# Three modulation vectors by matmuls in column quarters instead of sums on VectorE

## The chip, the cores and the metric

The kernel runs on one core of a Trainium2 chip. The metric is the device time of one execution, in microseconds (us); lower is better. PE is TensorE, DVE VectorE, ACT ScalarE, POOL GpSimd and SP the engine that issues most loads. "Before" is the kernel that the change starts from.

## The reference, cut to what matters

Two transformer blocks are computed for 512 tokens of width 1024. The first block takes a conditioning vector `c` and makes six modulation vectors of 1024 numbers from it. They shift, scale and gate what the attention and the expert layer see:

```python
c_act = jax.nn.silu(c)
mod = c_act @ w_ada[l] + b_ada[l]                  # 1024 x 6144 weights
sh_a, sc_a, g_a, sh_f, sc_f, g_f = jnp.split(mod, 6, axis=-1)
h = modulate(rmsnorm(x), sh_a, sc_a)               # h * (1 + scale) + shift
...                                                # windowed and latent attention
x = x + g_a[:, None, :] * (mixed @ w_out[l])
h = modulate(rmsnorm(x), sh_f, sc_f)
x = x + g_f[:, None, :] * peer(h, ...)
```

So `sh_a` and `sc_a` are needed at once, `g_a` (vector 2) at the output projection, `sh_f` and `sc_f` (3 and 4) at the norm behind it, and `g_f` (5) only at the end of the expert layer. All is fp32; most matmuls are made of three fp32r products of a split into a high and a low part (`mm3`, lines 199 to 201).

## The kernel before, in words

The tile `mod`, 128 x 48, holds the six vectors as columns: column m is numbers 128 m to 128 m + 127, eight columns to a vector. Each column is made on DVE. A row block of the transposed weights, 128 x 1024 (512 KB, the tile `wa`), is loaded by SP (`ada_dma`, line 491); one instruction multiplies it by the broadcast `silu(c)` in `cs` and sums along the row into the column (line 553 for columns 0 to 15, line 503 for the other 32). The bias is added later, a vector or more at a time (lines 738, 772, 817).

Columns 16 to 47 are made beside other work by the generator `ada_rest` (line 494). Each step of it issues one load and sums the tile loaded a step earlier, with two buffers; the sum is held behind the latest row maximum or up-projection product on DVE. `next(ada)` takes a step. The stages around it, in order:

- The latent up-projection (lines 642 to 664): eight query tiles `qu` of six 128x512 matmuls, eight `kup` of three and four `vup` of three, into eight PSUM banks that are used in turn. DVE multiplies each query tile by a table (line 649); the rotary part of the first attention's queries is done beside it, with copies by DMA. A step of `ada` after every second query tile.
- The first, windowed attention (`attend`, line 241, with names that begin with sw): 32 units, each a score tile, a row maximum on DVE, an exponential on ACT, a scaling on POOL, a transpose and, for two units together, the product with the values (line 329, `128*64`: each head of a pair writes one half of the output partitions). A step of `ada` after every eighth unit (`ADA_E`). `ps.then(sc=LA + 1, pt=2, po=5 - LA)` (line 666) hands the eight banks on, the one used longest ago first: five to scores, two to transposes, one to outputs.
- The second, latent attention (names with ml): the same 32 units with scores of 128x512 in fp32 (line 269). Beside it weights of the output projection are loaded and split, and `both` (line 728) takes a step of `ada` after every second of those steps. What is left of the 24 columns is made at the end (line 737).
- The output projection (`w_out`, line 751): two halves of four row blocks, each block 24 matmuls, then a scaling by `out_rstd` and `ga` and an addition to `x` on DVE (lines 761 and 762). `ga` is vector 2 as a row, made by `mod_row` (line 212). Two steps of `ada` a block, for columns 40 to 47; in the second half the norm of the block before follows (`norm2`, line 794), which transposes on PE and needs vectors 3 and 4.

Loads wait for a free buffer on SP's queue, in order; weights for `mm3` come through `Stream` (line 79) with four raw buffers, split on ACT and DVE (lines 111 and 112). The order on each engine is settled when the program is built, by a scheduler that goes by program order and by when it takes an instruction to be ready; the engine then works its queue in that order.

Of the kernel before, what the change touches and what calls it, by code (L numbers as in the profile page):

```python
# [9 lines left out]
FT = mybir.dt.float32  # L10
# [10 lines left out]
P = 128  # L21
# [24 lines left out]
GSCALE = 4096.0  # L46
WR, WH, SD = 4, 5, 3
RB = 1
ADA_E = 8
ADA1 = 40  # L50
LA = 4
ADA_U = 2
ADA_M = 2
OGP = 3
U_PRE = 4
B_END = 120
# [101 lines left out]
def body(ctx, tc, a):  # L158
# [3 lines left out]
    def pool(st, name, bufs=1, side="left", **kw):  # L162
        return st.enter_context(tc.tile_pool(name=name, bufs=bufs, side=side, reuse_waits="tile", **kw))
# [304 lines left out]
    rp = ExitStack()  # L468
    crow = cs[0:1]
    nc.sync.dma_start(crow, a["c"])  # L470
    i = A.activation(crow, crow, AF.Silu)
    with tc.issue_after(i.ins):

        A.activation(small.tile([P, 1], FT, name="warm0", tag="nss"), eps, AF.Sqrt)
# [14 lines left out]
    def ada_dma(pl, m, eng, bufs):  # L489
        wa = pl.tile([P, D], FT, name=f"wa{m}", tag="wa", bufs=bufs)  # L490
        eng.dma_start(wa, a["w_adaT"][m * P:(m + 1) * P, :])
        return wa

    def ada_rest(pl, ms, bufs=2):

        prev = []
        for m in list(ms) + [None] * (bufs - 1):
            if m is not None:
                prev.append((m, ada_dma(pl, m, nc.sync, bufs)))
            if m is None or len(prev) == bufs:  # L500
                n, w = prev.pop(0)
                with tc.issue_after(last["max"]):
                    V.scalar_tensor_tensor(w, w, 1.0, cs, op0=OP.mult, op1=OP.mult, accum_out=mod[:, n:n + 1])
            yield

    with ExitStack() as s1:
# [132 lines left out]
                    V.tensor_copy(km[64:, h], t[64:])  # L639


        ada = ada_rest(pada, range(16, ADA1))
        for h in range(8):
            if h % 2 == 0:
                w = ws.get(("qup", h // 2))
            pt = ps.tile([P, S], FT, name=f"qu{h}", tag="ps")
            c = slice(h % 2 * 256, h % 2 * 256 + 256)
            lin(pt, [(w[0][:, c], w[1][:, c])], 2, ALL, lambda k: lT[:, 0, k], lambda k: lT[:, 1, k])
            last["max"] = V.tensor_mul(qm[:, h], pt, tabm[:, 0]).ins
            if h % ADA_U == 0:  # L650
                next(ada, None)
        for h in range(8):
            if h % 4 == 0:
                w = ws.get(("kup", h // 4))
            pt = ps.tile([P, S], FT, name=f"kup{h}", tag="ps")
            c = slice(h % 4 * P, (h % 4 + 1) * P)
            mm3(pt, w[0][:, c], w[1][:, c], lT[:, 0, 2], lT[:, 1, 2], True, True)
            A.activation(km[:64, h], pt[:64], AF.Copy)
        w = ws.get(("vup",))
        for b in range(NB):  # L660
            pt = ps.tile([P, 512], FT, name=f"vup{b}", tag="ps")
            bl = slice(b * P, (b + 1) * P)
            mm3(pt, lT[:, 0, 2, bl], lT[:, 1, 2, bl], w[0], w[1], True, True)
            A.activation(vm[:, b], pt, AF.Copy)

    ps = ps.then(sc=LA + 1, pt=2, po=5 - LA)
    fa = ExitStack()
    pc = pool(fa, "pc", 2)

    def attn_done(half, pl):  # L670
        st = {}
# [27 lines left out]
    def zip_run(main, side, every=1):  # L699
        n = 0  # L700
        for _ in main:
            n += 1
            if n % every == 0:
# [5 lines left out]
                   lambda kt, h: va[:, kt, (h // 4) * 64:(h // 4) * 64 + 64],  # L709
                   [(j, j + 4) for j in range(4)], 64 ** -0.5, "sw", attn_done(0, pc),  # L710
                   mask=(identb, maskb), sink=vec[:, V_SINK:V_SINK + 8]), ada, ADA_E)
    fa.close()
    rq.close()
    r1 = ExitStack()
# [10 lines left out]

    wol = wo_loads()

    def both():
        while True:
            for i in range(ADA_M):  # L730
                next(wol, None)
                yield
            next(ada, None)
    zip_run(attend(pc, ps, lambda h: (qm[:, h], None), lambda h: (km[:, h], None),
                   lambda kt, h: vm[:, kt, h * 64:(h + 1) * 64],
                   [(2 * j, 2 * j + 1) for j in range(4)], 96 ** -0.5, "ml", attn_done(1, pc)), both())
    run(wol, ada)
    V.tensor_add(mod[:, 16:24], mod[:, 16:24], vec[:, V_BADA + 16:V_BADA + 24])
    fa.close()
    rp.close()  # L740

# [4 lines left out]
    ga = pd1.tile([P, D], FT, name="ga")  # L746
    mod_row(ps, "ps", ga, 16, "ga")
    rows_tiles(pd1, "wo", range(4, 8))
    ada = ada_rest(pd1, (*range(ADA1, 48),))

    def w_out(half, b):
        bl = slice(b * P, (b + 1) * P)
# [13 lines left out]
    for b in range(NB):  # L766
        take_rows("wo", 4 + b)
        next(ada, None)
        next(ada, None)
        w_out(0, b)  # L770
    next(ada, None)
    V.tensor_add(mod[:, 24:40], mod[:, 24:40], vec[:, V_BADA + 24:V_BADA + 40])
    V.tensor_scalar(mod[:, 32:40], mod[:, 32:40], 1.0, None, op0=OP.add)
    out_rstd[1] = out_rstd[1]("ps")
    r1.close()
# [15 lines left out]
    with ExitStack() as s2:  # L791
        pn = pool(s2, "pn", 2)

        def norm2(b):
            sq = pn.tile([P, D], BF, name=f"sq2{b}", tag="sq", bufs=1)
            ss = small.tile([P, 1], FT, name=f"ss2{b}", tag="nss")
            A.activation(sq, x[:, b], AF.Square, accum_out=ss)
            r = rstd(ss, 1, 1.0 / D, f"n2{b}")
            xn = pn.tile([P, D], FT, name=f"xn2{b}", tag="xn")
            V.tensor_scalar(xn, x[:, b], r, None, op0=OP.mult)  # L800

            def dst(k0, b=b):
                c = slice(b * P, (b + 1) * P)
                return hA[:, 0, k0:k0 + 4, c], hA[:, 1, k0:k0 + 4, c]
            transposed(pn, ps, xn, dst, mod[:, 32:40], mod[:, 24:32], f"n2{b}",
                       lambda k0: G if b < 3 and k0 == 0 else V)

        for b in range(NB):
            w_out(1, b)
            if b:  # L810
                norm2(b - 1)
            next(ada, None)
            next(ada, None)
        ws.upto(("qy", 0, 1), 0)
        norm2(NB - 1)
    run(ada)
    V.tensor_add(mod[:, 40:48], mod[:, 40:48], vec[:, V_BADA + 40:V_BADA + 48])
    s1.close()
    rm.close()

# [697 lines left out]
def _layout(inp):  # L1518
    i = {k: np.asarray(v) for k, v in inp.items()}
    con, tab = _constants()  # L1520
    wi = i["w_in"][0]
    qa, ka, va, ql, kvl, kr = np.split(wi, np.cumsum([512, 128, 128, 256, 128]), axis=1)
    order = np.concatenate([np.arange(h * 64, h * 64 + 64) for j in range(4) for h in (j, j + 4)])
    z64 = np.zeros((D, 64), wi.dtype)
    w_in = np.concatenate([ql, kvl, va, z64, kr, kr, ka, qa[:, order]], axis=1)
    qup = i["w_mla_q_up"][0].reshape(256, 8, 96)
    rp = qup[:, :, 64:]
    qup = np.concatenate([qup, rp[:, :, 16:], rp[:, :, :16]], axis=2).reshape(256, 1024)
    kvu = i["w_mla_kv_up"][0].reshape(128, 8, 128)
    kup = np.concatenate([kvu[:, :, :64], np.zeros_like(kvu[:, :, :64])], axis=2).reshape(128, 1024)  # L1530
    vup = kvu[:, :, 64:].reshape(128, 512)
    wi2 = i["w_in_2"][0]
    q2, k2, v2, u2 = np.split(wi2, [512, 640, 768], axis=1)

    half = np.arange(64).reshape(2, 2, 16).transpose(1, 0, 2).reshape(64)
    q2 = q2[:, order].reshape(D, 8, 64)[:, :, half].reshape(D, 512)
    k2 = k2.reshape(D, 2, 64)[:, :, half].reshape(D, 128)
    w_in2 = np.concatenate([q2, k2, v2, u2], axis=1)
    vecs = np.concatenate([
        _cols(i["b_ada"][0]), _cols(i["mla_q_norm"][0]), _cols(i["mla_kv_norm"][0]),  # L1540
        _cols(i["out_norm_swa"][0][order]), _cols(i["out_norm_mla"][0]), _cols(i["norm1_g_2"][0]),
        np.tile(i["q_norm_g_2"][0][half], 2)[:, None], np.tile(i["k_norm_g_2"][0][half], 2)[:, None],
        _cols(i["pool_b_2"][0]), _cols(i["pool_scale_2"][0]), _cols(i["norm2_g_2"][0]),
        np.broadcast_to(i["swa_sink"][0][None, :], (P, 8)),
    ], axis=1)
    assert vecs.shape == (P, NVEC)
    return {
        "x": i["x"][0], "c": i["c"], "vecs": vecs, "consts": con, "tabs": tab,
        "w_adaT": i["w_ada"][0].T, "w_in": w_in,
        "w_qup": _rows(_pack(qup)), "w_kup": kup, "w_vup": vup, "w_out": np.concatenate([i["w_out"][0][:512][order], i["w_out"][0][512:]], axis=0),  # L1550
        "w_query": _pack(i["w_peer_query"][0]),
        "subT": i["peer_sub_keys"][0].reshape(16, P, P).transpose(2, 0, 1).reshape(P, 2048),
        "uT": _pack(i["peer_expert_u"][0].T), "u": i["peer_expert_u"][0], "v": i["peer_expert_v"][0], "final_norm": i["final_norm"][None, :],
        "w_in2": _pack(w_in2), "pool_w": i["pool_w_2"][0], "w_out2": np.concatenate([i["w_out_2"][0][:512][order], i["w_out_2"][0][512:]], axis=0),
        "w_gate": _pack(i["w_gate_2"][0]), "w_up": _pack(i["w_up_2"][0]), "w_down": i["w_down_2"][0],
    }
# [17 lines left out]
```

## Time and profile before

| | |
|---|---|
| median of 3 runs | 2220.59 us (2214.14 to 2221.76) |
| the profiled execution | 2222.11 us |
| its span in the profile | 2220.3 us |
| busy: PE, PEld, DVE, ACT, POOL | 95%, 80%, 73%, 43%, 28% |
| mean granted clock of PE | 0.977 |
| HBM traffic | 366.66 MB read, 4.19 MB written |

The profile is one execution, taken by the hardware profiler. Its span runs from the first to the last instruction, and the execution's own time is 1.8 us longer. PE is busy with matmuls, PEld with loading their stationary operand, which overlaps. An fp32 matmul leaves two records in the trace, an fp32r one a single record. A row of a timeline or of a group names line, engine, operation, the tile written `<-` the tiles read, the columns of the array where PE is concerned (`128*64` is 128 rows and 64 columns), and the idle time before it with what ended it. The stages told above lie between 62 and 294 us of the 2220.

### The profile page before, as it was taken

What the parts mean: (1) busy time and instruction counts of PE and PEld (TensorE: products, weight loads), DVE (VectorE), ACT (ScalarE), POOL (GpSimd) and SP (SyncE); (2) the same over time, 40 slices, a digit from 0 to 9 for tenths busy, and PEclk for the clock granted to TensorE, in tenths of its full rate; (3) what the DMA queues carried; (4) which work ended last, traced back from release to release, by engine and by line L of the source; (5) the groups of instructions that cost most, each with busy time, mean ns of one, the idle gap of its engine ahead of it and who ended that gap; (6) DMA issues with size and microseconds to landing.
All of it is one profiled execution on the core that took longest, in us unless ns stands there. A gap on an engine that the chain in (4) does not pass through costs nothing.

```text
span 2220.3 us, 35038 instructions
## 1 busy us (share of the span) xinstructions
PE 2102.8 (95%) x12443; PEld 1771.4 (80%) x12443; DVE 1624.1 (73%) x3587; ACT 954.2 (43%) x1899; POOL 618.3 (28%) x553
## 2 busy tenths in 40 slices
PE   7999998888999999999999999999998999999999
PEld 5756787778888888888888888788887678888887
DVE  7779889997878997777799777777767865333322
ACT  4467342345435553333355433333353553333321
POOL 2245245564222113333312233333303420000000
PEclk9999999988999999999999999999999999999999
DMA  8515522231575558878855688888844221333332
GB/s 273 166 49 164 173 70 66 89 111 57 172 254 191 168 166 270 281 268 285 285 186 165 196 279 268 262 265 281 295 138 122 65 67 45 98 96 99 95 117 73
DMA packets 163634, 375.79 MB, mean 169 GB/s; under 512 B 18562, under 2 KB 22530, under 8 KB 163459
## 3 DMA queue, kind: packets, MB, share of 16 engines
q1 hardware_dynamic: 121058, 233.81, 31.6%
q0 software_dynamic: 36864, 134.23, 19.3%
q10 hardware_dynamic: 5536, 5.51, 0.9%
q8 instruction: 98, 1.61, 0.3%
q14 instruction: 78, 0.63, 0.1%
HBM read 366.66 MB, written 4.19 MB: 167 GB/s over the span
## 4 chain that ended last, share of the span: by engine, by line
PE 56%; DVE 16%; DMA 15%; issue 6%; ACT 4%; POOL 2%; ACTq 0%; SPq 0%; DVEq 0%; POOLq 0%
DMA vr<-in_v_dram,idx 7%; PE vac L200 4%; PE vac L201 4%; PE vac L199 4%; PE pA L199 4%; PE pA L200 4%; PE pA L201 3%; DMA wr<-in_uT_dram 3%; DMA ur<-in_u_dram,idx 3%; PE pd L201 2%; PE pd L200 2%; PE pd L199 2%; PE upp L201 2%; PE upp L199 2%; PE upp L200 2%
## 5 line engine op out<-in xcount | busy, mean ns | idle before, releaser
L111 ACT ACTIVATE wh<-wr 128x512 fp32r<-128x512 f32 x716 | 446.8, 631 | 760.4 <-DMA wr<-in_v_dram 162.1
L112 DVE TENSOR_TENSOR wl<-wr,wh 128x512 fp32r<-128x512 f32 x640 | 429.4, 695 | 286.4 <-ACT wh L111 270.2
L200 PE MATMUL vac<-wl,wwh 128*128 128x512 f32 x756 | 305.4, 404 | 32.7 <-DVE wl L112 32.3
L199 PE MATMUL pA<-hA,wh 128*128 128x384 f32 x928 | 318.1, 343 | 0.0
L201 PE MATMUL pA<-hA,wl 128*128 128x384 f32 x928 | 314.7, 339 | 0.0
L200 PE MATMUL pA<-hA,wh 128*128 128x384 f32 x928 | 313.9, 338 | 0.0
L199 PE MATMUL vac<-wh,wwh 128*128 128x512 f32 x756 | 304.3, 403 | 0.7 <-ACT wwh L1042 0.5
L201 PE MATMUL vac<-wh,wwl 128*128 128x512 f32 x756 | 299.5, 396 | 0.1
L1067 POOL DMA_INDIRECT ur<-in_u_dram,idx x128 | 160.5, 1254 | 383.3 <-DVE acc L1078 308.2
L1067 POOL DMA_INDIRECT vr<-in_v_dram,idx x128 | 155.3, 1213 | 338.2 <-DVE ur L1070 252.5
L200 PEld LDWEIGHTS vac<-wl,wwh 128*128 128x128 f32 x756 | 144.2, 191 | 73.5 <-DVE wl L112 49.2
L1078 DVE SCALAR_TENSOR_TENSOR acc<-vr,act,acc 128x1024 f32<-128x1024 f32 x127 | 162.7, 1281 | 46.7 <-DMA vr<-in_v_dram,idx 45.4
L1070 DVE SCALAR_TENSOR_TENSOR ur<-ur,hn 128x1024 f32<-128x1024 f32 x128 | 156.2, 1220 | 39.0 <-DMA ur<-in_u_dram,idx 39.0
L199 PEld LDWEIGHTS pA<-hA,wh 128*128 128x128 f32 x928 | 177.0, 191 | 4.1 <-ACT ga L1031 0.7
L200 PEld LDWEIGHTS pA<-hA,wh 128*128 128x128 f32 x928 | 177.0, 191 | 3.1
L201 PEld LDWEIGHTS pA<-hA,wl 128*128 128x128 f32 x928 | 176.6, 190 | 0.0
L201 PEld LDWEIGHTS vac<-wh,wwl 128*128 128x128 f32 x756 | 144.0, 190 | 30.1 <-DVE wwl L1043 0.8
L199 PEld LDWEIGHTS vac<-wh,wwh 128*128 128x128 f32 x756 | 144.1, 191 | 28.7 <-ACT wh L111 0.9
L112 POOL TENSOR_TENSOR wl<-wr,wh 128x512 fp32r<-128x512 f32 x76 | 101.9, 1352 | 74.6 <-ACT wh L111 71.7
L1042 ACT ACTIVATE wwh<-w 128x384 fp32r<-128x384 f32 x126 | 66.0, 524 | 117.2 <-DVE w L1035 115.0
L1008 PEld LDWEIGHTS <-oj 128*128 128x128 f16 x1152 | 83.2, 117 | 38.1 <-issue 16.4
L989 DVE TENSOR_TENSOR oj<-iT,ioth 128x1024 f16<-128x1024 f16 x144 | 106.0, 740 | 9.2 <-PE pG L1009 9.2
(697 smaller groups left out, 4319.7 us busy)
## 6 DMA issues: line engine op xcount, KB each, us to landing
wr<-in_uT_dram SPq DMA_DIRECT2D x256, 256.0 KB
wr<-in_v_dram SPq DMA_DIRECT2D x256, 256.0 KB
wa<-in_w_adaT_dram SPq DMA_DIRECT2D x48, 512.0 KB
wr<-in_w_gate_dram SPq DMA_DIRECT2D x44, 256.0 KB
wr<-in_w_up_dram SPq DMA_DIRECT2D x44, 256.0 KB
wr<-in_w_down_dram SPq DMA_DIRECT2D x44, 256.0 KB
wr<-in_w_in_dram SPq DMA_DIRECT2D x36, 256.0 KB
wr<-in_w_out_dram SPq DMA_DIRECT2D x32, 256.0 KB
```

Of the source, the lines that this page charges most:

```text
L111: self.nc.scalar.activation(hi, raw, AF.Copy)
L112: (lo_eng or self.nc.vector).tensor_tensor(lo, raw, hi.bitcast(FT), op=OP.subtract)
L199: T.matmul(out, lh, rh, start=start, stop=False)
L200: T.matmul(out, lh, rl, start=False, stop=False)
L201: return T.matmul(out, ll, rh, start=False, stop=stop).ins
L989: V.tensor_tensor(out, iT[:, q, tt].rearrange("p (s t) -> p s t", t=4)[:, :, None].to_broadcast([P, GS // 4, w, 4]), ioth[:, None, j0:j0 + ...
L1008: T.matmul(pt[:, t, :n], oj[:, t // 4, :, t % 4], o[:, :, 1], start=True, stop=False)
L1042: A.activation(wh, w, AF.Copy)
L1067: G.indirect_dma_start(out=r, out_offset=None, in_=a[kind], in_offset=bass.IndirectOffsetOnAxis(ap=idx[:, j:j + 1], axis=0))
L1070: V.scalar_tensor_tensor(r, r, 1.0, hn, op0=OP.mult, op1=OP.mult, accum_out=act[:, j:j + 1])
L1078: V.scalar_tensor_tensor(acc, r, act[:, j:j + 1], acc, op0=OP.mult, op1=OP.add)
```

## The change

`ada_pe` makes vectors 2, 3 and 5 on PE. For a half of a vector (512 numbers) it loads eight tiles of the weights as they are, 128 x 512 (256 KB, tile `wv`), and multiplies each with a column of `silu(c)` spread to 32 columns as the stationary operand. Four tiles at a time go to the four quarters of 32 output partitions of one bank (a group, `g` from 0 to 3); a second group adds to it. ACT copies the bank to a row tile, and four matmuls against a 128 x 1 column `sel`, with ones at rows 0, 32, 64 and 96, add up the quarters and turn the row into four columns of `mod` (here called flips); DVE adds the bias. A half takes three steps of the generator: group, group and copy, flips. There are five `wv` buffers, and the row takes one of them as well. Vectors 2 and 3 are made in the up-projection, with a step after each query tile and every second `kup` tile and the last one behind `vup`; vector 5 is made in the output projection with one step a block. Vector 4 (columns 32 to 39) stays on DVE and is made in the first attention, a step after every fourth unit; the second attention has none.

```diff
-ADA_E = 8
-ADA1 = 40
+ADA_E = 4
...
+    ccol = keep.tile([P, KD], FT, name="ccol")
+    nc.scalar.dma_start(ccol, a["c_cols"])
     i = A.activation(crow, crow, AF.Silu)
+    i = A.activation(ccol, ccol, AF.Silu)
+    sel = keep.tile([P, 1], FT, name="sel")
+    V.memset(sel, 0.0)
+    for g in range(4):
+        V.memset(sel[32 * g:32 * g + 1], 1.0)
...
+    def ada_pe(pl, tag, vs, bufs=4):
+        todo = [(v, n, k) for v in vs for n in range(2) for k in range(KD)]
+        loaded = {}
+        def load():
+            if todo:
+                v, n, k = u = todo.pop(0)
+                loaded[u] = w = pl.tile([P, 512], FT, name=f"wv{v}{n}{k}", tag="wv", bufs=bufs + 1)
+                nc.sync.dma_start(w, a["w_ada"][k * P:(k + 1) * P, v * D + n * 512:v * D + (n + 1) * 512])
+        for _ in range(bufs):
+            load()
+        for v in vs:
+            for n in range(2):
+                for k0 in range(0, KD, 4):
+                    yield
+                    if k0 == 0:
+                        pt = ps.tile([P, 512], FT, name=f"ad{v}{n}", tag=tag)
+                    for g in range(4):
+                        T.matmul(pt[32 * g:32 * g + 32], ccol[:, k0 + g:k0 + g + 1].to_broadcast([P, 32]),
+                                 loaded.pop((v, n, k0 + g)), start=k0 == 0, stop=k0 == KD - 4)
+                    for g in range(4):
+                        load()
+                row = pl.tile([P, 512], FT, name=f"adr{v}{n}", tag="wv", bufs=bufs + 1)
+                A.activation(row, pt, AF.Copy)
+                yield
+                pc = ps.tile([P, 4], FT, name=f"adc{v}{n}", tag=tag)
+                for k in range(4):
+                    T.matmul(pc[:, k:k + 1], row[:, k * P:(k + 1) * P], sel, start=True, stop=True)
+                c = v * KD + n * 4
+                V.tensor_add(mod[:, c:c + 4], pc, vec[:, V_BADA + c:V_BADA + c + 4])
...
-        ada = ada_rest(pada, range(16, ADA1))
+        ada = ada_pe(pada, "ps", (2, 3))
...
-            if h % ADA_U == 0:
-                next(ada, None)
+            next(ada, None)
...
             A.activation(km[:64, h], pt[:64], AF.Copy)
+            if h % 2:
+                next(ada, None)
...
+        run(ada)
...
     pc = pool(fa, "pc", 2)
+    ada = ada_rest(pc, range(32, 40))
...
+    run(ada)
     fa.close()
...
-                   [(2 * j, 2 * j + 1) for j in range(4)], 96 ** -0.5, "ml", attn_done(1, pc)), both())
-    run(wol, ada)
-    V.tensor_add(mod[:, 16:24], mod[:, 16:24], vec[:, V_BADA + 16:V_BADA + 24])
+                   [(2 * j, 2 * j + 1) for j in range(4)], 96 ** -0.5, "ml", attn_done(1, pc)), wol)
+    run(wol)
+    V.tensor_add(mod[:, 32:40], mod[:, 32:40], vec[:, V_BADA + 32:V_BADA + 40])
...
-    ada = ada_rest(pd1, (*range(ADA1, 48),))
+    ada = ada_pe(pd1, "ps", (5,))
...
         take_rows("wo", 4 + b)
         next(ada, None)
-        next(ada, None)
         w_out(0, b)
-    next(ada, None)
-    V.tensor_add(mod[:, 24:40], mod[:, 24:40], vec[:, V_BADA + 24:V_BADA + 40])
...
             next(ada, None)
-            next(ada, None)
         ws.upto(("qy", 0, 1), 0)
```

The weights are given to the kernel in both layouts, `w_adaT` and `w_ada`, and `c` as columns too (`c_cols`). The number of steps beside the output weights in the second attention changes with `both`: they now advance with every unit.

## Rows read from the trace of the kernel before

**Rows 1.** Page: PE's busy time and share; GB/s in 40 equal slices of the span.

```profile
PE 2102.8 (95%) x12443; PEld 1771.4 (80%) x12443; DVE 1624.1 (73%) x3587; ACT 954.2 (43%) x1899; POOL 618.3 (28%) x553
...
GB/s 273 166 49 164 173 70 66 89 111 57 172 254 191 168 166 270 281 268 285 285 186 165 196 279 268 262 265 281 295 138 122 65 67 45 98 96 99 95 117 73
```

**Rows 2.** Windows by stage: length, PE, PEld, DVE, ACT, POOL busy, clock, DMA, GB/s.

```profile
62.00:97.00 35.00, 35.00 (x157) 27.82 (x155) 25.53 (x49) 14.86 (x40) 8.07 (x6) 1.00 0.48 152
97.00:102.00 5.00, 1.36 (x5) 0.78 (x5) 5.00 (x9) 1.89 (x4) 1.96 (x1) 0.86 0.50 157
102.00:108.00 6.00, 6.00 (x16) 4.70 (x16) 4.86 (x8) 2.99 (x7) 0.17 (x1) 0.55 0.73 214
109.30:165.50 56.20, 54.25 (x375) 32.67 (x376) 41.66 (x163) 36.51 (x127) 23.15 (x34) 0.91 0.15 44
...
172.00:228.50 56.50, 56.49 (x447) 38.41 (x448) 51.72 (x134) 40.13 (x91) 29.97 (x31) 1.00 0.56 178
228.50:263.50 35.00, 35.00 (x158) 28.70 (x157) 32.21 (x52) 11.39 (x21) 9.33 (x6) 1.00 0.59 188
```

**Rows 3.** Windows of line 503 alone: length, DVE busy (instructions), clock, DMA, GB/s.

```profile
62.00:109.30 47.30, 3.67 (x6) 0.93 0.51 157
109.30:165.50 56.20, 6.56 (x10) 0.91 0.15 44
165.50:228.50 63.00, 21.99 (x32) 1.00 0.54 171
228.50:294.00 65.50, 11.02 (x16) 0.96 0.40 133
```

**Rows 4.** Chain of waits, second attention: start us, us, piece.

```profile
185.59 1.72 PE mlsc L269 x4
187.31 0.87 PE mlpt L309 x8
188.18 1.02 PE mlpo L329 x16
```

**Rows 5.** Chain of waits, between the two attentions.

```profile
166.18 1.14 DVE wa L503 x2
```

**Rows 6.** Timeline of PE, up-projection: start us, us, instruction, idle before.

```profile
82.81 0.80 PE L199 MATMUL qu<-lT,wh 128*128 128x512 f32 x1
...
99.45 0.47 PE L199 MATMUL kup<-lT,wh 128*128 128x512 f32 x1 [2.32 <-DVE qm L649]
...
102.30 0.63 PE L200 MATMUL kup<-lT,wh 128*128 128x512 f32 x1
102.72 0.63 PE L201 MATMUL kup<-lT,wl 128*128 128x512 f32 x1
...
109.30 0.39 PE L264 MATMUL swsc<-maskb,identb 128*128 128x256 bf16 x2
```

**Rows 7.** Timelines of SP's queue and ACT: two load issues and a use.

```profile
76.25 19.01 SPq L491 DMA_DIRECT2D wa<-in_w_adaT_dram  x3
...
232.72 0.93 SPq L93 DMA_DIRECT2D wr<-in_w_out_dram  x2
...
235.45 1.29 ACT L111 ACTIVATE wo6h<-wr 128x512 fp32r<-128x512 f32 x2 [2.68 <-DMA wr<-in_w_out_dram]
```

**Rows 8.** Timeline of PE: sums of squares, four matmuls of one moving column.

```profile
250.96 0.95 PE L694 MATMUL oss<-ones,osq 128*128 128x1 f32 x8
```

**Rows 9.** Chain of waits, then timeline of PE, before the first norm.

```profile
258.48 1.63 DVE wa L503 x2
...
266.71 1.09 PE L226 MATMUL n20pt<-ident,xn 128*128 128x128 f32 x8 [2.89 <-DVE xn L800]
...
268.30 0.63 PE L199 MATMUL wo<-wo6h,mixT 128*128 128x512 f32 x1
268.73 0.63 PE L200 MATMUL wo<-wo6l,mixT 128*128 128x512 f32 x1
```

**Rows 10.** Timeline of ACT at the start.

```profile
9.38 0.30 ACT L185 ACTIVATE rs_un<-ss,eps 128x2 f32<-128x2 f32 x1 [3.05 <-DVE sq L527]
```

More of the change, by code (lines that the diff above doesn't have):

```diff
@@ L48 @@
 RB = 1
-ADA_E = 8
-ADA1 = 40
+ADA_E = 4
 LA = 4
-ADA_U = 2
-ADA_M = 2
 OGP = 3
@@ L726, in body @@
     wol = wo_loads()
[L728 to L732, printed above, removed]
-            next(ada, None)
     zip_run(attend(pc, ps, lambda h: (qm[:, h], None), lambda h: (km[:, h], None),
                    lambda kt, h: vm[:, kt, h * 64:(h + 1) * 64],
-                   [(2 * j, 2 * j + 1) for j in range(4)], 96 ** -0.5, "ml", attn_done(1, pc)), both())
-    run(wol, ada)
-    V.tensor_add(mod[:, 16:24], mod[:, 16:24], vec[:, V_BADA + 16:V_BADA + 24])
+                   [(2 * j, 2 * j + 1) for j in range(4)], 96 ** -0.5, "ml", attn_done(1, pc)), wol)
+    run(wol)
+    V.tensor_add(mod[:, 32:40], mod[:, 32:40], vec[:, V_BADA + 32:V_BADA + 40])
     fa.close()
@@ L812, in body @@
             next(ada, None)
-            next(ada, None)
         ws.upto(("qy", 0, 1), 0)
@@ L816, in body @@
     run(ada)
-    V.tensor_add(mod[:, 40:48], mod[:, 40:48], vec[:, V_BADA + 40:V_BADA + 48])
     s1.close()
@@ L1548, in _layout @@
         "x": i["x"][0], "c": i["c"], "vecs": vecs, "consts": con, "tabs": tab,
-        "w_adaT": i["w_ada"][0].T, "w_in": w_in,
+        "w_adaT": i["w_ada"][0].T, "w_ada": i["w_ada"][0], "c_cols": i["c"].reshape(KD, P).T, "w_in": w_in,
         "w_qup": _rows(_pack(qup)), "w_kup": kup, "w_vup": vup, "w_out": np.concatenate([i["w_out"][0][:512][order], i["w_out"][0][512:]], axis=0),
```

## The prediction

> **What bounds the kernel now.** I read the page first, then busy time by stage, then the same view for the moved line alone, then the chain of waits and the timelines of the stages touched. The page says PE, 95% of the span [rows 1]; that is a mean, so each stage is read alone [rows 2]. From 62 to 97 and from 228.5 to 263.5 us PE is busy without a gap; in the second attention (172 to 228.5) as well. DVE is close behind: 51.72 of 56.5 us there, 32.21 of 35 in the output projection. The gaps that PE has are after the up-projection (1.36 busy of 5.0 from 97 to 102, then a granted clock of 0.55, mostly the lower level of 1.2 GHz) and in the norm behind 263.5. So nearly every microsecond put on PE here lasts, and one taken off DVE counts only where PE waits for DVE.
>
> **What moves.** 24 of the 32 later sums leave DVE. They stand 3, 5, 16 and 8 in the four stages (a sum is two instructions in the view) [rows 3]; after the change the counts are 0, 8, 0, 0. DVE loses 43.24 x 24/32 = 32.4 us. PE gains 12 groups of four matmuls and 6 sets of four flips. SP issues 48 loads of 256 KB where it issued 24 of 512 KB: 32 of them, 8 MB, now fall in the up-projection.
>
> **Price of a group.** The nearest 128x512 fp32 matmul is the second attention's score: four records are two matmuls, 1.72 us, so 0.86 each [rows 4]. Four in turn would be 3.44. The probability-times-value matmuls use half the columns each, alternating: 16 records take 1.02 us, while 8 full-width records of the same length take 0.87 [rows 4]. So halves overlap almost fully, 64 ns against 109 a record. I take quarters as doing the same: 0.95 a group, with 3.44 as the other end and 0.86 as the lower one. A set of flips is four matmuls with one moving column, as in the sum-of-squares row: 0.95 [rows 8].
>
> **Up-projection (A).** PE work added: 8 x 0.95 + 4 x 0.95 = 11.4 us. What can hide it: the 3.64 us gap and the slow clock behind it. Matmuls there start 0.42 apart [rows 6], against 35.0/157 = 0.22 before 97 [rows 2]; over some 12 of them that is 2.4. So 6.0 is hidden, and the three sums that made DVE late (3.67 us [rows 3], kup waiting for DVE qm [rows 6]) go too. By PE alone A ends 5.4 later.
>
> But the loads set a longer pace. There are five weight buffers: one tile is asked for ahead, the other three of a group only when the group before has released theirs. From issue to use a 256 KB load took 232.72 to 235.45 = 2.73 us [rows 7]; no slice of the page moves more than 295 GB/s [rows 1], so two more behind it take 0.9 each. So a group that finds PE early ends 2.73 + 1.8 + 0.9 = 5.4 after the one before; where PE waits at each matmul in turn, the releases are staggered and the next gap is about 2.73 + 0.9 + 0.9 = 4.5. First group: PE takes up the first up-projection at 82.81 [rows 6], two of them are 12 x 0.22 = 2.7, and the group ends at 86.4; its loads can leave at 76.25 as the first wa does [rows 7], so they are there. Seven gaps, four of 5.4 and three of 4.5, give 121.5 for the eighth group. PE runs its queue in order, so up-projections behind a waiting matmul wait too, and the last accumulators sit in the banks that the first attention's first scores and outputs take: the first score, now at 109.30 [rows 6], comes after the copy of the last row, at about 122. That is +12.7; the scheduler may put groups a little earlier, so **+12**, between +5.4 (loads always in time) and +25.4 (quarters in turn: 8 x 2.5 more). SP's own queue costs nothing: its w_out loads behind are for the second attention.
>
> **First attention (B).** Three sums more at 6.56/5 = 1.31 are 3.9 us of DVE, which has 14.5 us free there [rows 2, 3]. Nothing if each falls in a gap, 3.9 if each is met; the stage already loses clock (0.91 granted), and a worse placement could cost as much again. Behind a sum on DVE stand the row maximum and the reciprocal, and POOL's scaling waits for those. **+1.5**, from 0 to +8.
>
> **Second attention (C).** PE is busy 56.49 of 56.50, so 16 sums less shorten it little: one sum of 1.14 lies in the chain at 166.18 [rows 5], just before the first output is scaled; another 1 for fewer collisions. The output weights are split every third unit instead of every fourth or so: the same work. **-2**, from 0 to -4.
>
> **Output projection and norm (D).** PE gains 4 x 0.95 + 2 x 0.95 = 5.7. It loses the wait of 2.89 before the first norm's transposes, for which DVE was late with a sum of 1.63 in the chain, and the slow stretch after it (starts 0.43 apart, eight of them, 1.6) [rows 9]: 4.5. Left +1.2, less up to 2 for a DVE that is not behind in the last norm; the steps are 24 matmuls of 0.22 apart, 5.3 us, so gaps of 5.4 are about hidden, +3 if not. **+0.5**, from -4 to +4.
>
> The rest: a small load and a Silu on ACT at the start lie in ACT's 3.05 us wait for DVE [rows 10], and would cost about 1 us without it; five tiny memsets are on an idle DVE; six row copies on ACT (two such passes take 1.29 [rows 7]) and six small adds on DVE lie beside PE. Zero.
>
> Sum: 12 + 1.5 - 2 + 0.5 = +12.0 on the profiled execution's 2222.11 (span 2220.3): 2234.1. The median of the runs shown is 1.5 below that execution, so I forecast **2232.5 us**.
>
> **Rivals.**
> - *Loads in time.* A costs PE's 5.4 only: 2226. For it: SP's queue is nearly empty then. Against: five buffers for groups of four. 0.20.
> - *Not slower: DVE and its DMA pace D.* The first norm's transposes wait for DVE, behind a sum of 1.63 [rows 9]; 11.02 us of sums leave this stage [rows 3]. If DVE's row and not PE's sets it, and the loads of A are in time, the sum is 5.4 + 1.5 - 2 - 11.0 = -6.1: 2214.5. It decides where PE has slack before 263.5; against it, PE shows none [rows 2]. 0.15.
> - *The clock.* After 3.64 us without work PE was granted 0.55 of its clock from 102 to 108 and lost 2.4 us, 0.65 per idle microsecond. In A the forecast leaves PE idle for 122 - 82.8 - 20.4 - 11.4 = 7.4 (20.4 is its present work there, 26.5 less 6.0): another 5 us, 2238. 0.13. The Trainium skill says the same against this change: TensorE: Matmul & The Clock Gate, "Loop structure matters more than you think", calls a long wait for a DMA between matmuls the bad loop, because PE then drops to half its clock. By that rule the sum would be 2238, by the stretch before 97, where PE waits for nothing and keeps 1.00, 2232.5.
> - *No overlap of quarters.* 3.44 a group: A +25.4, D +10 more, 2257. Against: the halves. 0.08.
>
> **Chances.** The forecast has 0.42; 0.02 is something else. Half a per cent, 11.1 us, is about what a measurement of this kernel tells from no change: borders 2209.5 and 2231.7. The forecast lies just above the upper one, so 0.29 of its 0.42 is slower; with the clock 0.13 and no overlap 0.08, slower 0.50. Same: the other 0.13, loads in time 0.20, 0.08 of the DVE case: 0.41. Faster: 0.07 of the DVE case and the rest, 0.09. Range 2212 to 2246: it leaves out no overlap, the faster part of the DVE case and the rest, 0.17. The likeliest case alone is 2226 to 2240.
>
> **What will show it.** Right: in the changed profile PE waits for DMA on the w_ada tiles between 86 and 122, groups some 5 us apart, eight records of a group in about 0.9 us; the first score near 122; the second attention still about 56 us; no 2.9 us gap before the first norm. Wrong: the first score before 115 (loads in time), group records in a row of 0.43 (no overlap), or matmuls before the norm spreading out less than 5.7 us (DVE paced D).

## The result and the profile after

The changed kernel took **2252.05 us** (median of five runs, 2247.52 to 2264.91), the kernel before 2220.42 in runs on the same chip: ratio 1.0164, interval 1.0137 to 1.0191. It is 31.6 us slower. The forecast was 2232.5 with a range to 2246: the direction was right, the size was not.

The profiled execution is the longest of the five, 2264.91 us. Its page, against [rows 1]:

```profile
PE 2144.3 (95%) x12587; PEld 1780.0 (79%) x12587; DVE 1595.3 (71%) x3548; ACT 958.7 (42%) x1906; POOL 612.0 (27%) x553
```

PE is busy for 41.5 us more, DVE for 28.8 less, and PE's share has not moved. As in the forecast, each stage is read alone. Four marks cut the part that the change touches: the first row maximum of the first attention (swmx), the first and the last of the second (mlmx), and the transposes of the last norm (n23pt). They are the first and last start in the view of one tile:

```profile
L276 DVE TENSOR_REDUCE swmx<-swsc x32: 404/478/558, 138.4 to 186.3; 128x1 f32<-128x256 f32 x16, 128x1 f32<-128x384 f32 x16
...
L276 DVE TENSOR_REDUCE mlmx<-mlsc x32: 667/691/693, 191.2 to 250.8; 128x1 f32<-128x512 f32 x32
...
L223 PE MATMUL n23pt<-ident,xn x8: 272/273/327, 322.1 to 322.9; 128*128 128x128 f32 x8
...
L196 PE MATMUL vac<-wh,wwh x756: 388/392/632, 605.3 to 1704.3; 128*128 128x512 f32 x189
```

The same marks of every profiled run, in us, each column the length from one mark to the next (A up-projection with all ahead of it, B first attention, C second, D output projection and norm; "to vac" is the routing stage, up to the first `vac` matmul of the expert loop, and "loop" is that loop). The two kernels were profiled twice:

| run | A | B | C | D | n23pt at | to vac | loop |
|---|---|---|---|---|---|---|---|
| before | 110.3 | 49.1 | 60.8 | 68.7 | 288.9 | 283.2 | 1090.6 |
| before, again | 109.6 | 45.1 | 60.7 | 68.8 | 284.2 | 280.7 | 1086.6 |
| after | 138.4 | 52.8 | 59.6 | 71.3 | 322.1 | 283.2 | 1099.0 |
| after, again | 138.9 | 53.0 | 59.7 | 70.4 | 322.0 | 282.3 | 1089.4 |
| groups by one load | 121.8 | 53.9 | 58.1 | 70.4 | 304.2 | 281.6 | 1093.9 |
| nine buffers | 135.5 | 53.9 | 58.1 | 70.4 | 317.9 | 282.3 | 1088.8 |
| one strip | 138.7 | 52.3 | 58.1 | 82.2 | 331.3 | 283.1 | 1089.6 |
| vector 5 on VectorE | 138.9 | 51.2 | 58.1 | 67.7 | 315.9 | 284.3 | 1097.8 |
| vector 5 alone on PE | 109.6 | 45.1 | 60.8 | 70.1 | 285.6 | 283.1 | 1093.1 |
| vector 5 late | 110.5 | 45.0 | 61.2 | 62.9 | 279.6 | 286.9 | 1092.6 |
| vector 5 later | 109.8 | 45.1 | 60.8 | 62.9 | 278.6 | 287.8 | 1099.9 |
| no sums in A, eight in B | 103.4 | 51.8 | 63.7 | 70.9 | 289.8 | 282.4 | 1089.1 |
| both | 103.1 | 54.7 | 63.6 | 63.4 | 284.8 | 286.5 | 1092.2 |
| no sums in A, B as before | 104.6 | 55.9 | 60.8 | 64.0 | 285.3 | 286.9 | 1099.4 |

A, C and D of the same kernel repeat within 1 us; B differs by 4 in the kernel before, and the loop, which no edit here touches, by 13 over all runs. So the totals of single runs scatter by several us, and the marks tell more. The loss of 33.2 us at the last norm is **A +28.1, B +3.7, C -1.2, D +2.6**. Of the 42.8 us by which the profiled executions differ, another 8.4 are the loop, which was 1089.4 in the repeat. Against the repeat of the kernel before, B is +7.7 and not +3.7; the reason comes below.

**Where A's 28 us are.** PE is busy 55.48 of 56.40 us there, and 25.13 of them are the new matmuls alone. The window of A, then windows of PE's new tile alone, the up-projection and the output projection:

```profile
82.00:138.40 56.40, 55.48 (x204) 24.05 (x203) 20.12 (x36) 15.45 (x25) 5.45 (x4) 1.00 0.57 174
...
82.00:138.40 56.40, 25.13 (x64) 3.33 (x64) 2.39 (x4) 1.00 0.57 174
...
261.00:322.10 61.10, 5.11 (x32) 0.89 (x32) 1.17 (x2) 1.00 0.42 138
```

64 records are 32 matmuls, eight groups of four. Four groups in the output projection take 5.11 us, eight in the up-projection 25.13. The timeline of PE shows why. First the up-projection, then the output projection (start, length, instruction):

```profile
106.89 0.40 PE L198 MATMUL qu<-lT,wl 128*128 128x512 f32 x1
107.22 1.04 PE L519 MATMUL ad<-wv,ccol 128*32 128x512 f32 x2
108.19 0.50 PE L196 MATMUL kup<-lT,wh 128*128 128x512 f32 x1
108.53 0.39 PE L197 MATMUL kup<-lT,wh 128*128 128x512 f32 x1
108.76 0.40 PE L198 MATMUL kup<-lT,wl 128*128 128x512 f32 x1
109.09 1.04 PE L519 MATMUL ad<-wv,ccol 128*32 128x512 f32 x2
110.06 0.51 PE L196 MATMUL kup<-lT,wh 128*128 128x512 f32 x1
...
266.63 0.40 PE L198 MATMUL wo<-wo3h,mixT 128*128 128x512 f32 x1
266.95 1.06 PE L519 MATMUL ad<-wv,ccol 128*32 128x512 f32 x8
267.95 0.50 PE L196 MATMUL wo<-wo0h,mixT 128*128 128x512 f32 x1
268.28 0.39 PE L197 MATMUL wo<-wo0l,mixT 128*128 128x512 f32 x1
```

Call an unbroken run of the new matmuls in PE's queue a spell. At 266.95 the four quarters of a group (eight records) stand together in one spell and take 1.06. At 107.22 and 109.09 a spell is one quarter (two records), and it takes 1.04 all the same. Each spell also costs at its ends: from 266.63 to 268.28 are 1.65 us where two starts 0.23 apart would be 0.46, so a spell costs PE **1.19 us, whether it holds one quarter or four**. In A the 32 quarters stand in 24 spells. Each has its own load, and the scheduler goes by when it takes an instruction to be ready; the first experiment shows that with one load for a group the quarters of a group meet. Separate loads alone do not spread them: in the output projection, where a step comes some 7 us after the one before, all four groups stand whole.

24 x 1.19 = 28.6, and the four sets of flips are 4.0 us of PE there; less the 3.64 us that PE waited before [rows 2], 28.9, against 28.1 in the marks. The match is in part luck, for two terms that this sum leaves out nearly cancel. The slow clock of before, 2.4 us by the forecast, is gone. And A now holds work of the next stage: PE starts the first scores at 129.88, 8.6 us ahead of the first row maximum (1.0 before), and has spent 3.0 us more on scores when A ends. The first row maximum waits for the score at 137.58, which stands behind the last flips (timeline of PE):

```profile
129.88 0.28 PE L261 MATMUL swsc<-maskb,identb 128*128 128x256 bf16 x1
...
136.67 1.05 PE L528 MATMUL adc<-sel,adr 128*128 128x1 f32 x8 [0.69 <-ACT adr L524]
137.58 0.27 PE L261 MATMUL swsc<-maskb,identb 128*128 128x256 bf16 x1
```

### The profile page after: what moved, and what is told of

Its sections match the earlier page's. It is cut to its first block, busy times and chain, and to the rows that moved or that the text cites. A ratio compares the mean times of both kernels' runs of the same rounds, so it can differ in the third digit from the quotient of the medians.

```text
span 2262.8 us, 35350 instructions
## 1 busy us (share of the span) xinstructions
PE 2144.3 (95%) x12587; PEld 1780.0 (79%) x12587; DVE 1595.3 (71%) x3548; ACT 958.7 (42%) x1906; POOL 612.0 (27%) x553
## 4 chain that ended last, share of the span: by engine, by line
PE 60%; DVE 14%; DMA 13%; issue 6%; ACT 3%; POOL 3%; SPq 0%; ACTq 0%; DVEq 0%; POOLq 0%
DMA vr<-in_v_dram,idx 8%; PE vac L197 4%; PE vac L196 4%; PE vac L198 4%; PE pA L196 4%; PE pA L197 4%; PE pA L198 3%; DMA ur<-in_u_dram,idx 2%; PE pd L197 2%; PE pd L196 2%; PE pd L198 2%; PE upp L198 2%; PE upp L197 2%; PE upp L196 2%; PE gatep L197 2%
## 5 line engine op out<-in xcount | busy, mean ns | idle before, releaser
L1109 DVE SCALAR_TENSOR_TENSOR acc<-vr,act,acc 128x1024 f32<-128x1024 f32 x127 | 162.8, 1282 | 49.1 <-DMA vr<-in_v_dram,idx 49.0
L196 PEld LDWEIGHTS vac<-wh,wwh 128*128 128x128 f32 x756 | 144.5, 191 | 28.6 <-ACT wwh L1073 1.1
L1039 PEld LDWEIGHTS <-oj 128*128 128x128 f16 x1152 | 83.2, 117 | 38.2 <-issue 16.6
```

The costliest lines, as they stand in the source:

```text
L196: T.matmul(out, lh, rh, start=start, stop=False)
L1039: T.matmul(pt[:, t, :n], oj[:, t // 4, :, t % 4], o[:, :, 1], start=True, stop=False)
L1109: V.scalar_tensor_tensor(acc, r, act[:, j:j + 1], acc, op0=OP.mult, op1=OP.add)
```

## The experiments

### One load for a group

```diff
-w = pl.tile([P, 512], ...); nc.sync.dma_start(w, a["w_ada"][k * P:(k + 1) * P, ...])     # one tile
+w = pl.tile([P, 4, 512], ...); nc.sync.dma_start(w, a["w_ada"][k * P:(k + 4) * P, ...])  # a group
```

(`pada` stands behind `km` and is closed before the first attention, and `lat` is in `p0`, to make room: 18 KB a partition instead of 10. The next kernel has the same layout.)

> Edit: the four tiles of a group come as one tile by one load of 1 MB (two such buffers), so that the four matmuls of a group are ready at one moment and stand next to each other in PE's queue: 8 spells of them in the up-projection instead of 24. Theory (the order of PE's queue: each spell costs PE about 1.2 us, however many of the four quarters it holds, by the trace of the changed kernel: 1.00 for the spell in the output projection and 0.09 + 0.10 at its two ends): 16 spells less are 19 us less; first attention's first exponential near 119 instead of 138; total about 2233 (2229 to 2238). Rival 1 (loads: five buffers of 256 KB set the pace): the memory is 8 tiles instead of 5, so some gain, but the same as in the run with nine single buffers. Rival 2 (quarters do not overlap on the chip, each costs about 0.9 wherever it stands): 2252, spells of about 3.4 us.

Measured: 2236.62 us (2234.77 to 2239.85), ratio to before 1.0073, interval 1.0048 to 1.0097. Eight spells in A, each a whole group as in the first four rows; the last two stand behind the first score (timeline of PE):

```profile
105.61 0.40 PE L196 MATMUL kup<-lT,wh 128*128 128x512 f32 x1
105.93 1.06 PE L521 MATMUL ad<-wv,ccol 128*32 128x512 f32 x8
106.93 0.50 PE L197 MATMUL kup<-lT,wh 128*128 128x512 f32 x1
107.26 0.40 PE L198 MATMUL kup<-lT,wl 128*128 128x512 f32 x1
...
114.44 0.28 PE L261 MATMUL swsc<-maskb,identb 128*128 128x256 bf16 x1
...
118.16 1.06 PE L521 MATMUL ad<-wv,ccol 128*32 128x512 f32 x8
...
120.01 1.05 PE L528 MATMUL adc<-sel,adr 128*128 128x1 f32 x8 [0.41 <-ACT adr L524]
```

And the windows of the new tile, which hold all eight:

```profile
82.00:122.00 40.00, 8.52 (x64) 1.25 (x64) 2.40 (x4) 1.00 0.81 270
```

A is 121.8 instead of 138.4, 16.6 less; the last norm is 17.9 earlier and the median 15.4 lower, a little under the theory's 19 (the total lies in its range). Work and bytes are the same; the new matmuls went from 25.13 to 8.52 us of PE. So the order of PE's queue carried about half of the loss. Of the 11.5 us that A is still longer than before, 5.1 have passed at the first score (109.30 before, 114.44 here); the other 6.4 pass between that score and the first row maximum, with the last two groups and flips in between. Whether an earlier place for these would win them back was not tried.

### Nine single buffers

```diff
-def ada_pe(pl, tag, vs, bufs=4):
+def ada_pe(pl, tag, vs, bufs=8):
```

> Edit: nine buffers of one tile instead of five, each still loaded alone. In PE's queue the quarters of the up-projection then stand in 20 spells instead of 24 (one of seven, most of one). Theory (order of PE's queue): 4 spells less at 1.2 are 5 us less: about 2247 (2243 to 2251). Rival 1 (five buffers and the loads set the pace): the pace goes, as much gain as with one load for a group: about 2230 or less. Rival 2 (no overlap of quarters): 2252.

Measured: 2253.75 us (2249.93 to 2257.04), ratio 1.0158, interval 1.0132 to 1.0184. The total shows no gain and misses the 2247, though by the marks the last norm is 4.2 us earlier, about what four spells less are worth. The total is nearest to rival 2, but quarters that meet do overlap here as well, seven of them in 1.92 us (timeline of PE):

```profile
129.67 1.92 PE L519 MATMUL ad<-wv,ccol 128*32 128x512 f32 x14
```

What the run settles is rival 1: with the memory of the run above but a load for each tile, 4.2 of its 17.9 us come. In the changed kernel itself PE waited 0.5 us for a `wv` tile in all. So waiting for loads did not set the pace of PE on the chip. That the loads, as the scheduler took them to land, set the order when the program was built is the likely reading; the scheduler's own times are not on record.

### One strip instead of quarters

```diff
-T.matmul(pt[32 * g:32 * g + 32], ...)
+T.matmul(pt[:32], ...)                 # all eight of a half add into the same 32 partitions
```

> Edit: the kernel with one load for a group, but all eight matmuls of a half add into the same 32 output partitions instead of four quarters; the flips take 32 rows. The same number of matmuls of the same size. Theory (quarters overlap on the chip, four in 1.06 us; in one strip they come in turn at 0.86 or more): a group is 3.4 to 3.6 us instead of 1.06, 8 groups in the up-projection and 4 in the output projection: 12 x 2.4 = 29 us more, to about 2265 (2258 to 2270). Rival (no overlap comes from the quarters, matmuls to one strip run as closely): 2237, groups of 1.06.

Measured: 2261.81 us (2255.13 to 2264.75), ratio 1.0193, interval 1.0169 to 1.0218. A group in the timeline of PE:

```profile
104.57 3.62 PE L521 MATMUL ad<-wv,ccol 128*32 128x512 f32 x8
```

The windows of the tile, up-projection and output projection:

```profile
82.00:139.00 57.00, 29.14 (x64) 6.29 (x64) 2.36 (x4) 1.00 0.58 189
262.00:332.00 70.00, 14.48 (x32) 3.19 (x32) 1.16 (x2) 1.00 0.36 130
```

Against the run with one load for a group, a group is 3.62 instead of 1.06 and D is 11.8 longer. So quarters do overlap on this chip, and the forecast's rival without overlap falls. But compare 29.14 us in A with the 25.13 of the changed kernel: placed in 24 spells, the quarters saved 4 of the 20.6 us that they save in groups.

### Vector 5 on VectorE again, and vector 5 alone on PE

```diff
-    ada = ada_pe(pd1, "ps", (5,))                     # first: the changed kernel without this
+    ada = ada_rest(pd1, (*range(40, 48),))
...
-    ada = ada_rest(pd1, (*range(ADA1, 48),))          # second: the kernel before with it
+    ada = ada_pe(pd1, "ps", (5,))
```

> Edit: the changed kernel, but vector 5 is made by sums on VectorE in the output projection, as in the kernel before; vectors 2 and 3 stay on PE in the up-projection. Theory (nearly all of the loss is in the up-projection; in the output projection what PE gains and what it no longer waits for cancel): 2252, within 3 us of the changed kernel. Rival (vector 5's matmuls cost their 4 x 1.2 + 2 x 0.9 = 6.6 us on PE and nothing comes back): 2245. Rival (VectorE set the output projection's pace, and vector 5 on PE saves time): 2256 or more.

> Edit: the kernel before with vector 5 alone moved to PE in the output projection; the 24 sums of vectors 2 to 4 stay where they were. Theory (gain and loss cancel there): 2220, within 3 us of the kernel before. Rival (the matmuls cost 6.6 us and nothing comes back): 2227. Rival (VectorE set the pace there): 2214 or less.

Measured: 2253.06 us (2251.37 to 2254.26; ratio 1.0148, interval 1.0123 to 1.0173) and 2223.07 (2216.06 to 2232.53; 1.0018, interval 1.0000 to 1.0037). Both within 3 us of their starting points, so nearly all of the loss lies with the other vectors, 2 to 4, and by the marks in A. The marks are finer: D is 67.7 with vector 5 on DVE and 70.4 to 71.3 with it on PE beside the change, 68.7 and 70.1 beside the kernel before. Vector 5 on PE costs D 1.4 to 3.6, not the forecast's 0.5. PE is busy 70.90 of D's 71.30 us: the wait before the first norm is gone, as forecast, and a little more work stands in its place.

### Looking for a version that beats both

Three edits of the kernel before: vector 5 on PE in the routing stage behind the norm (late; `query`, `level2` and the tiles `top`, `cand` and `best` belong to that stage), no sums in A, and both together. "Late" also drops the steps of the output projection.

```diff
-    ada = ada_rest(pd1, (*range(ADA1, 48),))          # late
...
+    ada = ada_pe(p1, "ps", (5,))
     query(0, 1)
     for h in range(8):
...
         level2(h, top, tif)
+        next(ada, None)
...
-ADA_E = 8                                             # no sums in A
+ADA_E = 4
...
-        ada = ada_rest(pada, range(16, ADA1))
...
+    ada = ada_rest(pc, range(16, 24))                 # first attention
...
+    ada = ada_rest(pc, range(24, ADA1))               # second attention
```

> Edit: the kernel before, with vector 5 moved from VectorE in the output projection to PE in the routing stage behind the first norm (a step after each head; quarters in groups of four), where VectorE is busy throughout and PE about four fifths. Theory (the 11 us of sums in the output projection held up the norm; PE's time in the routing stage is free): the wait of 2.9 before the first norm and the slow clock behind it go, about 4 less: 2216 (2213 to 2219). Rival 1 (PE sets the output projection's pace and nothing comes off): 2220, within 2. Rival 2 (matmuls with loads in the routing stage delay the queries that VectorE waits for): 2224 or more.

> Edit: the kernel before with all its sums on VectorE, but none in the up-projection: vector 2 in the first attention, a step after every fourth unit, vectors 3 and 4 in the second; vector 5 as before. Theory (the three sums in the up-projection make VectorE late by 2.3 us there and cost a slow stretch of PE behind it; three more sums in the first attention cost at most 2): first exponential near 107 instead of 110, total 2218 (2214 to 2221). Rival (the first attention with eight sums is what cost the changed kernel its 3.7 us there): 2222 to 2225.

> Edit: the two edits of the two runs before together. Theory: the gains add, 2214 (2210 to 2217), faster than both kernels. Rival 1 (the first attention's eight sums take the gain of the up-projection away): 2217 to 2221. Rival 2 (PE sets every stage's pace): 2220.

Measured against 2215.86 for the kernel before: 2216.26 us (ratio 0.9996, interval 0.9974 to 1.0017), 2221.84 (1.0032, 1.0012 to 1.0051) and 2218.74 (1.0012, 0.9996 to 1.0028). None is faster, and the marks tell what became of each gain. D fell by 5.8 with vector 5 late, a clear gain; but the stage behind it grew by 3.7. A fell by 6.9 without its sums; but B, C and D grew by 2.7 (6.7 against the repeat), 2.9 and 2.2.

Two more, to win back what was lost: vector 5 from the third head on (`if h > 1`), and the same with no sums in A but only three in B, 16 in C and the last five of vector 4 in D.

> Edit: the kernel before with vector 5 on PE in the routing stage, as in the run before, but from the third head on, when VectorE no longer waits for the first scores. Theory (VectorE lost 3.6 us there because the first two groups stood before scores that it waited for): that stage as long as before, and with the 5.8 us of the output projection kept, the first vac matmul near 566 (562 to 568, by the clock of the first attention), total 2213 (2209 to 2217). Rival (any matmuls there delay VectorE): the stage again 3 to 4 us longer, 2217 or more.

> Edit: the kernel before without sums in the up-projection; the first attention keeps its step after every eighth unit (3 sums), the second its 16, the first half of the output projection makes the last 5 of vector 4, and vector 5 is made on PE in the routing stage from the third head on. Theory (a sum costs time where VectorE or PE waits for it and nothing elsewhere): up-projection 7 us shorter (as the run with no sums there), first and second attention as before, output projection 3 to 5 shorter, routing stage at most 1 longer: the first vac matmul near 562 instead of 572, total 2210 (2206 to 2214). Rival (what is taken out of one stage comes back in the next, as in the run with none in the up-projection and eight in the first attention): the first vac matmul at 568 to 572, total 2216 to 2221.

Measured against 2216.49: 2221.50 us (1.0013, interval 0.9987 to 1.0039) and 2224.19 (1.0024, 1.0002 to 1.0046). Both theories failed and both rivals came true by the marks; the second total lies 3 us above its rival's range. With vector 5 later the routing stage is still 4.6 longer. The waits of DVE between the first and the last `best`, in the kernel before and with vector 5 later:

```profile
DVE best L897 <- POOL cand L889: 0.9, 2, 0.4
...
DVE best L930 <- POOL cand L922: 4.2, 5, 2.4
DVE top L911 <- ACT scs L908: 0.8, 1, 0.8
```

The kernel before has 0.9 us of the first and none of the second. Why POOL brings `cand` later was not tried. Without sums in A, the 5.7 us of A come back in B (+6.8), and there the row that shows it is the clock. Windows of 6 us of that last kernel:

```profile
98.00:104.00 6.00, 4.60 (x22) 3.44 (x22) 4.34 (x8) 4.41 (x9) 1.28 (x1) 1.00 0.29 77
104.00:110.00 6.00, 4.24 (x23) 2.46 (x22) 3.56 (x13) 5.97 (x17) 0.48 (x1) 0.88 0.00 0
110.00:116.00 6.00, 6.00 (x19) 3.46 (x19) 2.71 (x15) 2.36 (x10) 2.19 (x4) 0.50 0.00 0
116.00:122.00 6.00, 6.00 (x34) 3.98 (x32) 1.96 (x11) 3.21 (x14) 1.53 (x3) 0.50 0.00 1
122.00:128.00 6.00, 6.00 (x56) 3.78 (x54) 4.23 (x19) 4.13 (x15) 1.72 (x4) 0.99 0.01 3
```

And the kernel before, from its end of the up-projection and from the middle of the first attention:

```profile
98.00:104.00 6.00, 3.23 (x8) 2.33 (x9) 6.00 (x11) 3.69 (x7) 2.12 (x1) 0.72 0.59 173
104.00:110.00 6.00, 6.00 (x25) 4.50 (x23) 3.48 (x6) 3.06 (x7) 0.00 (x0) 0.71 0.46 132
110.00:116.00 6.00, 5.74 (x34) 3.22 (x30) 5.06 (x23) 5.46 (x18) 1.11 (x3) 1.00 0.00 0
140.00:146.00 6.00, 4.62 (x25) 2.76 (x23) 3.11 (x13) 3.11 (x14) 3.42 (x5) 0.63 0.27 87
146.00:152.00 6.00, 6.00 (x29) 3.56 (x31) 2.10 (x9) 1.05 (x3) 0.93 (x2) 0.52 0.00 0
```

Before, PE stands still while kup waits for DVE (3.23 busy of 6), and the lower clock falls on the last matmuls of the up-projection; the pause at the first attention's start (5.74 of 6) is short, and no slow stretch follows it. Take the wait in A away, and PE comes to the first attention sooner, waits there for the first exponentials (4.24 of 6), and then runs 12 us at 0.50, in the attention. The slow stretch has moved, not gone: all nine profiles in which that wait of 3.2 to 3.6 us is gone or shorter have one in the first 20 us of the first attention, and none of the five with it has. The changed kernel shows it here:

```profile
138.00:144.00 6.00, 4.33 (x15) 2.24 (x15) 4.79 (x21) 3.62 (x15) 0.94 (x2) 0.72 0.00 0
144.00:150.00 6.00, 6.00 (x25) 3.86 (x25) 2.56 (x11) 2.79 (x11) 2.71 (x4) 0.50 0.26 88
150.00:156.00 6.00, 6.00 (x34) 3.53 (x34) 2.12 (x11) 1.48 (x5) 1.56 (x3) 0.64 0.00 1
156.00:162.00 6.00, 5.87 (x52) 3.74 (x51) 5.98 (x25) 5.22 (x19) 2.94 (x4) 1.00 0.30 90
```

That the pause brings the fall is not shown. In the run with one strip the clock fell in the same stage, though PE had no wait over 0.31 us between 130 and 150:

```profile
138.00:144.00 6.00, 5.69 (x33) 3.40 (x32) 4.66 (x20) 4.45 (x16) 0.74 (x2) 1.00 0.01 1
144.00:150.00 6.00, 6.00 (x27) 3.62 (x27) 3.23 (x15) 2.90 (x11) 2.90 (x4) 0.56 0.27 87
```

### Both kernels again

> No edit: the kernel before, profiled once more, to see which of the marks of the stages repeat. Theory (queue order settles a stage's length but for the clock, which depends on how long PE pauses): first row maximum of the first attention again within 1 us of 110.3, second attention 60.8 and output projection 68.7 within 1 us; the first attention 45 or 49, by whether PE's clock falls a second time near 140. Rival (the marks scatter by several us in every stage, and differences between single profiles show nothing): differences over 2 us in the other stages too.

> No edit: the changed kernel, profiled once more. Theory: first row maximum of the first attention again within 1 us of 138.4, with a slow stretch of the clock right behind it and the first attention 51 to 54; the expert loop (first to last vac matmul), 1099 in the first profile, may differ by 5 or more. Rival (the scatter of the marks is several us in every stage): first maximum off by more than 2 us.

The marks repeat as the theory has it (the table); the loop took 1089.4 where it was 1099.0. In the repeat of the kernel before, the clock did not fall near 140 and B is 45.1, as in three edits that leave B's order alone:

```profile
140.00:146.00 6.00, 4.87 (x40) 3.12 (x40) 4.02 (x18) 2.78 (x11) 2.60 (x4) 1.00 0.29 87
```

That second slow stretch is 4 us that come and go with nothing changed. So what the change costs in B is better read against this repeat: 7.7 to 7.9 us.

## Why the prediction was wrong, point by point

- **What bounds the kernel: right in the main.** PE in every stage touched; of the 28.8 us that DVE was freed of, C gave back 1.2, and D up to the 5.8 that the run with vector 5 late shows.
- **Price of a group, 0.95: the step that failed.** The size was right for four quarters that stand together (1.06, and 1.19 with the ends). But the term took for granted that they would: "8 x 0.95" counts groups, and PE paid for spells, 24 of them: 28.6 us in A where the term has 7.6. The forecast's rival with 3.44 a group was put at 2257 (its terms add up to 2256), near the result, for a reason that the one-strip run excludes. The first-order question was not whether the hardware overlaps quarters, but whether the queue lets them meet. The Trainium skill (TensorE: Matmul & The Clock Gate, "Measured speedup vs the span model") says that packed tiles cost one duration plus some 4 ns for each further one; the trace agrees, 1.04 for one quarter and 1.06 for four. So a quarter by itself is priced like a group.
- **The loads' pace in A: wrong.** No gap of 5 us between groups, and 0.5 us of waiting for `wv` in all. The likely way in which the loads worked is the order instead: the scheduler spread the quarters by the times at which it took the loads to land, and the chip then ran that order almost without a wait. The end of the stage was half right: the first row maximum does come behind the last row's copy, though the first scores do not. +12 became +28.1.
- **"So 6.0 is hidden": half wrong.** The wait for DVE went, but a slow stretch turned up at the start of the first attention: B was priced +1.5 for its sums and came out +3.7, and +7.7 against the repeat of before. With groups by one load, A is 11.5 longer and A and B together 16.3. The Trainium skill (the same page, "Loop structure matters more than you think") says that a long wait for a DMA between matmuls makes PE go cold. The traces here do not bear on that directly: the clock was 0.50 behind a stretch with 4.33 of 6 us busy, but its longest wait was 1.57 us and not for a DMA, and in the one-strip run it fell behind 5.69 of 6. The forecast's clock rival put this into A, where the clock stayed at 1.00.
- **C: right in sign.** -1.2 for -2 (-2.7 in four other runs): PE sets its pace, and 22 us of sums less bring 1 to 3. The splitting of the output weights advances with every unit in both kernels, since `both` only adds steps of `ada`; the change of its pace that was told ahead of the result does not take place.
- **D: +2.6 for +0.5.** PE is busy for 6.8 us more there (64.14 to 70.90), against 5.7 forecast; the 2.9 us wait and the slow clock went as said. With the sums gone and nothing in their place (vector 5 late) D is 5.8 shorter, within the 4.5 to 6.5 of the forecast. So it is the matmuls that cost more: 7.2 to 8.4 by the marks.

Of the 28.1 + 3.7 - 1.2 + 2.6 = 33.2 us, 16 spells too many are priced at 16 x 1.19 = 19, and the run with one load for a group won back 17.9. The 15.3 that are left in it are A +11.5, B +4.8, C -2.7 and D +1.7: in A and D the matmuls in their groups, with the late first row maximum, and in B the slow stretch and three more sums, whose shares no run separates.

## What to carry to other kernels

Price work added to TensorE by the spells that it will form in the queue, not by its matmuls: ask what makes each of them ready, and if small matmuls are to run side by side, let one event (one load, one tile) release them all. A wait taken out may only move the slow clock into the next stage, as it did here, so look one stage on. And where PE is busy throughout, work taken off VectorE is worth next to nothing: no division of these sums tried here beat the kernel before.

## What was not expected of the hardware

A lone matmul of a quarter, 32 columns, takes as long as four side by side (1.04 and 1.06 us), and going from the fp32r matmuls to it and back costs another 0.19. An up-projection full of single spells keeps PE at 1.00 of its clock throughout, with records that say "busy" for 55.48 of 56.40 us: the busy share does not tell such time from useful time. And the granted clock fell to 0.50 behind a stretch in which PE was still busy for 4.24 of 6 us and its longest wait was 1.76, and to 0.56 behind one of 5.69 with a longest wait of 0.31, while 4.87 of 6 was followed by no fall in the repeat of the kernel before. What sets these falls off stays open.
